# One-hot products of the second layer's further blocks over 128 partitions instead of 32 or 64

## The chip, the cores and the metric

The kernel runs on one core of a Trainium2 chip. The metric is the device time of one execution in microseconds. The weights (about 360 MB read per execution) come from HBM. Engines are named as in the profile: PE is TensorE's matrix products, PEld its loads of the stationary operand, DVE is VectorE, ACT ScalarE, POOL GpSimd, SP SyncE, which issues the weight transfers.

## The reference

A trunk of two layers over 256 latent tokens and 256 context tokens, 1024 channels wide. Each layer mixes tokens (a gated MLP, latent attention and a linear recurrence in parallel), then runs a mixture of 16 experts, and each half ends in a layer norm over alpha * x + gate * sublayer. Only the latent tokens of the second layer's output are returned, so the second layer's experts see 256 tokens. The router picks one group of four experts for a token and two experts in it:

```
best = argmax(group_score); _, local = top_k(in_group, 2)
expert_idx = best * 4 + local;  w = 2.5 * score / sum(score)
out = sum over experts of combine[:, e] * ((silu(h @ wg[e]) * (h @ wu[e])) @ wd[e])
```

The kernel computes each expert for its own tokens alone, all in float32.

## The kernel before

Tokens are sorted by their pair of experts, and a one-hot product gathers them, channel-major, into XgT. An expert's tokens are then a run of at most 256 slots, worked in blocks: slots 0 to 63 always (block 0), then 32, 32, 64 and 64 slots (blocks 1 to 4), each further block only if the expert has that many tokens. This is decided on the chip by a branch (`tc.If` in `over`, L1611) that PE, ACT, DVE and POOL all take. Each block runs through five steps: `take` copies its slots (L1510, L1512), `up` multiplies them with the gate and up weights (L1533), `gate` applies silu and the product (L1539, L1540), `turn` transposes (L1547, L1548), and `down` multiplies with the down weights (L1564). For a block of 32 slots, four groups of 32 columns of the array work side by side in `up` and `down`.

In the second layer the expert's output goes straight back to the tokens. `down` multiplies it with the residual gate (L1578) into rows of a tile y, `place_rows` builds a matrix S (slots by tokens) that holds a token's weight in the row of its slot and zero elsewhere (L1474, L1475), and `scatter` adds S transposed times y to the accumulators cps (L1481): for two token tiles and two halves of the channels, four products of 512 columns. Each is recorded as two instructions, since it is float32. For block 0, two experts share an S of 128 rows, 64 each, and one `scatter` serves both. A further block has its own So and its own y, two tiles named yo; it writes rows 64 up to 64 plus its size, and `scatter` runs over these rows only. So is used once before, by `token_rows`, for the rows of the second layer's weights (L1466, L1467).

PE goes in program order: up products of the next expert (in part), turn and down of this expert, its further blocks inside the branch, the rest of the next expert's up products. `feed` lets SP issue the weight pages (L1284, 1 MB each) into a ring of 16; a page is loaded again when the products that read it before are done. In the profile the tile names of weights are pg and pb, yo appears under its pool's name x, and cps under acc. After the last expert, a layer norm of the accumulators writes the output (L1720 to L1730).

Of the kernel before, what the change touches and what calls it, by code (L numbers as in the profile page):

```python
# [89 lines left out]
def build(tc, I, out, dbg=None):  # L90
    nc = tc.nc
    with ExitStack() as ctx:
        _body(ctx, tc, nc, I, out, dbg or {})


def _body(ctx, tc, nc, I, out, dbg):
# [6 lines left out]
    pe, act, dve, pool, sp = nc.tensor, nc.scalar, nc.vector, nc.gpsimd, nc.sync  # L103
# [14 lines left out]
    def xtile(dt=F):  # L118
        return XP.tile([128, 512], dt, tag="x", name="x")
# [206 lines left out]
    for l in range(NL):  # L326
# [24 lines left out]
        def k2(name="k2", dt=F):  # L351
            return K2.tile([128, 512], dt, tag="k2", name=name)
# [509 lines left out]
        if first:  # L862
# [16 lines left out]
            for q in range(4):  # L879
                h, o = q // 2, q % 2  # L880
                t_ada.append([])
                for i in (1, 0):
                    t = ST.tile([128, 2048], F, tag="adaw", name="adaw", bufs=6)
# [60 lines left out]
        for n in range(2):  # L944
            t = k2("wbd")
# [7 lines left out]
        for n, un in enumerate(units):  # L953
# [15 lines left out]
            if n == LNAT and not first:  # L969
                for m in range(2):  # L970
                    for j, op in ((2, ALU.mult), (3, ALU.add)):
                        t = k2("ln2")
# [319 lines left out]
        if not first:  # L1292
            sc = W2.tile([128, 4, 96], F, name="sc", bufs=1)
            S_ = [W2.tile([128, 256], F, tag="S", name="S") for _ in range(2)]
            So = W2.tile([128, 256], F, name="So", bufs=1)
# [162 lines left out]
        def token_rows():  # L1458

            dve.tensor_tensor(wt[:, 1, :T], wt[:, 1, :T], wt[:, 0, :T], op=ALU.subtract)  # L1460
            for n, (col, dst) in enumerate(((pos, posrow), (wt[:, 0], w0row), (wt[:, 1], wdrow))):
                t = (S_ + [So])[n]
                ps = (yp_[0][:, 0:256], yp_[0][:, 256:512], pt_[0][:, 256:512])[n]
                for a in range(T):
                    s = slice(128 * a, 128 * a + 128)
                    dve.tensor_scalar(t[:, s], ident, col[:, a:a + 1], None, op0=ALU.mult)  # L1466
                    pe.matmul(ps[:, s], onesf, t[:, s], start=True, stop=True, skip_group_check=True)  # L1467
            act.activation(posrow, yp_[0][:, 0:256], AF.Copy)
            act.activation(w0row, yp_[0][:, 256:512], AF.Copy)
            act.activation(wdrow, pt_[0][:, 256:512], AF.Copy)  # L1470

        def place_rows(dst, rows, pcol, fcol):

            dve.scalar_tensor_tensor(dst[rows], wdrow[rows], fcol[rows], w0row[rows], op0=ALU.mult, op1=ALU.add)  # L1474
            dve.scalar_tensor_tensor(dst[rows], posrow[rows], pcol[rows], dst[rows], op0=ALU.is_equal, op1=ALU.mult)  # L1475

        def scatter(S, y, rows, stop=False):
            for i in tiles:
                a = tiles.index(i)
                for n in range(2):  # L1480
                    pe.matmul(cps[i, n], S[rows, 128 * a:128 * a + 128], y[n][rows], start=False, stop=stop,  # L1481
                              skip_group_check=True)
# [7 lines left out]
        else:  # L1490
            gu_ = [sd(), sd()]
            pt_, yp_ = [sd()], [sd()]
            yo = [xtile(), xtile()]
# [20 lines left out]
        def bufs_of(e, b):  # L1514
            q = ORDER.index(e)
            if not first:
                h = slice(64, 128) if b else slice(0, 64)
                return gu_[q % 2], hh_[b % 2 if b else q % 2][h], pt_[0], yp_[0], hT_[min(b, 1)], None
            if b == 0:
                return gu_[q % 2], hh_[q % 2][0:64], pt_[0], yp_[0], hT_[0], y_[q % 2][0:64]  # L1520
            return gu_[2 + b % 2], hh_[b % 2][64:128], pt_[1], yp_[1], hT_[1], y_[(q + b) % 2][64:64 + blocks[b][1]]
# [28 lines left out]
        def down(e, b):  # L1550
            r0, Mb = blocks[b]
            ng = 128 // Mb
            N = 1024 // ng
            _, _, _, yp, hT, y = bufs_of(e, b)
            wd = [streams[l, "wd", e, h].rearrange("p (k c) -> p k c", k=2) for h in range(2)]
            hT3 = hT.rearrange("p (a b) -> p a b", b=64)
            for f in range(4):
                if Mb == 64:
                    lt = hT3[:, f, :]
                else:  # L1560
                    half, c = divmod(f, 2)
                    lt = hT3[:, c, 32 * half:32 * half + 32]
                for j in range(ng):
                    pe.matmul(yp[Mb * j:Mb * j + Mb, :N], lt, wd[f // 2][:, f % 2, N * j:N * j + N],  # L1564
                              start=f == 0, stop=f == 3, skip_group_check=True)
            if not first:
                q = ORDER.index(e)
                if b == 0:
                    rows = slice(64 * (q % 2), 64 * (q % 2) + 64)
                    yt = [y_[q // 2 % 2][:, 512 * n:512 * n + 512] for n in range(2)]  # L1570
                else:
                    rows, yt = slice(64, 64 + Mb), yo
                if b:
                    place_rows(So, rows, pcol[:, b, e:e + 1], fcol[:, b, e:e + 1])
                for j in range(ng):
                    n, c = divmod(N * j, 512)
                    part = slice(Mb * j, Mb * j + Mb)
                    dve.tensor_tensor(yt[n][rows, c:c + N], yp[part, :N], g2[n][part, c:c + N], op=ALU.mult)  # L1578
                if b:
                    scatter(So, yo, rows)  # L1580
                return
            for j in range(ng):
                src, dst = yp[Mb * j:Mb * j + Mb, :N], y[:, N * j:N * j + N]
                if j % 2:
                    dve.tensor_copy(dst, src)  # L1585
                else:
                    act.activation(dst, src, AF.Copy)  # L1587
            if b == 0:
                rows = slice(1024 + ORDER.index(e) * M0, 1024 + ORDER.index(e) * M0 + Mb)
            else:  # L1590
                o, n = (2048, 512) if e % 4 == 3 else (0, 1024)
                rows = ds(nc.values_load(ci[0:1, 1, e:e + 1], engines=[ET.Pool], min_val=0,
                                         max_val=max(n - (r0 - M0) - Mb, 0)) + (o + r0 - M0), Mb)
            st = pool.dma_start(ys[rows, :], y)
            for o in stores:
                tc.declare_no_dep(st.ins, o.ins, reason="other rows")
            stores.append(st)

        def over(e, b, v, following):

            def before(last):
                if last:
                    following()
                if b > 1:
                    turn(e, b - 1)
                down(e, b - 1)

            if b == len(blocks):
                before(True)
                return  # L1610
            with tc.If(v > blocks[b][0], label=f"further_{l}_{ORDER.index(e)}_{b}") as c:  # L1611
                if b + 1 < len(blocks):
                    foretell(ORDER.index(e), v, b + 1)
                wide = b + 1 < len(blocks) and blocks[b + 1][1] == 64
                if b + 1 < len(blocks) and not wide:
                    take(e, b + 1)
                up(e, b, range(8))
                if wide:
                    take(e, b + 1)
                gate(e, b)  # L1620
                before(False)
                over(e, b + 1, v, following)
            with c.Else():
                before(True)
# [46 lines left out]
        for q, e in enumerate(ORDER):  # L1671
# [8 lines left out]
            if q == 0 and not first:  # L1680
                token_rows()
# [237 lines left out]
```

## Time and profile before

| | us |
|---|---|
| median of three timed runs | 1500.34 |
| their lowest and highest | 1496.33, 1503.78 |
| profiled execution, its own time | 1505.39 |
| its span, first to last instruction of the program | 1503.7 |
| PE busy, PEld busy | 1334.2, 843.9 |
| DVE, ACT, POOL busy | 739.6, 449.3, 138.2 |
| second layer's experts, from about / to about | 1225, 1495 |

The profile is of one execution. A row of a timeline merges like instructions that follow each other: start on the span, duration from the first start to the last end, engine, line, operation, output and inputs, shapes and count; in square brackets the time for which the engine was idle before, and what ended it. "issue" stands where nothing that the profile shows was waited for. The granted clock (PEclk) is 1.00 at 2.4 GHz and 0.50 at 1.2 GHz.

### The profile page before, as it was taken

Reading aid. Unit: us, or ns where it says so; the run is one execution under the profiler, and the core shown is the slowest. Engines: PE = TensorE matmul, PEld = TensorE weight load, DVE = VectorE, ACT = ScalarE, POOL = GpSimd, SP = SyncE. Lnnn points to the kernel's source line nnn. Section 1 sums busy time; section 2 is a strip of 40 time slices with the busy share of each in tenths; the row PEclk is TensorE's granted clock in tenths of the full one; section 3 lists DMA queues with packets and bytes.
Section 4 is the critical chain, followed back from the end, with each engine's and each line's share of the span. In section 5 each row is a group of like instructions: output and inputs, shape, how many; then the busy total and the mean of one; then the engine's idle time right before and its main releaser. Section 6 shows DMA issues by size and latency. Waiting matters only on the chain. (4 is left out here: it accounts for less than half of the span.)

```text
span 1503.7 us, 21798 instructions
## 1 busy us (share of the span) xinstructions
PE 1334.2 (89%) x8147; PEld 843.9 (56%) x8147; DVE 739.6 (49%) x1448; ACT 449.3 (30%) x781; POOL 138.2 (9%) x251
## 2 busy tenths in 40 slices
PE   5999889999999978988988779869998889989976
PEld 4777667777787853323333368546767753333322
DVE  3376774553466671323222456887676762222323
ACT  2437533333241221210111173764434320000000
POOL 0020000000022210000000441100002110000000
PEclk9999999999999988998989889999999999898988
DMA  9494332332353377998897646535535579988891
GB/s 377 172 376 173 135 143 89 114 143 85 112 191 118 131 321 300 418 414 346 330 386 280 214 131 231 192 130 200 219 118 205 180 309 403 371 325 340 353 402 49
DMA packets 56816, 358.15 MB, mean 238 GB/s; under 512 B 7316, under 2 KB 8116, under 8 KB 17920
## 3 DMA queue, kind: packets, MB, share of 16 engines
q1 hardware_dynamic: 46048, 320.83, 54.7%
q0 software_dynamic: 9808, 33.39, 6.6%
q8 instruction: 111, 1.82, 0.5%
q10 hardware_dynamic: 720, 1.06, 0.2%
q14 instruction: 129, 1.06, 0.2%
HBM read 342.63 MB, written 12.62 MB: 236 GB/s over the span
## 5 line engine op out<-in xcount | busy, mean ns | idle before, releaser
L373 PE MATMUL acc<-whi,pg 128*128 128x512 f32 (+1 forms) x424 | 173.6, 409 | 0.0
L374 PE MATMUL acc<-wlo,pg 128*128 128x512 f32 (+1 forms) x424 | 165.7, 391 | 4.6 <-DVE wlo L361 4.3
L375 PE MATMUL acc<-whi,pg 128*128 128x512 f32 (+1 forms) x424 | 164.8, 389 | 0.0
L361 DVE TENSOR_TENSOR wlo<-pg,whi 128x1024 fp32r<-128x1024 f32 x104 | 127.0, 1222 | 71.5 <-ACT whi L360 71.2
L360 ACT ACTIVATE whi<-pg 128x1024 fp32r<-128x1024 f32 x104 | 109.5, 1055 | 83.5 <-PE acc L375 54.8
L1564 PE MATMUL sd<-pg,lnv 128*64 128x512 f32 (+1 forms) x416 | 78.0, 566 | 21.2 <-issue 11.0
L374 PEld LDWEIGHTS acc<-wlo,pg 128*128 128x128 f32 x424 | 80.6, 190 | 24.5 <-DVE wlo L361 8.7
L373 PEld LDWEIGHTS acc<-whi,pg 128*128 128x128 f32 x424 | 80.6, 190 | 21.8 <-issue 5.2
L375 PEld LDWEIGHTS acc<-whi,pg 128*128 128x128 f32 x424 | 80.4, 190 | 15.9
L1564 PE MATMUL sd<-pb,lnv 128*64 128x512 f32 (+1 forms) x416 | 70.7, 543 | 14.8 <-ACT lnv L1548 7.1
L1533 PE MATMUL acc<-pg,xs 128*64 128x512 f32 x256 | 71.4, 655 | 13.8 <-DMA pg<-in_wg 4.3
L1539 ACT ACTIVATE hh<-sd 64x512 f32<-64x512 f32 (+1 forms) x18 | 10.2, 568 | 198.7 <-PE sd L1533 198.7
L1533 PE MATMUL acc<-pb,xs 128*64 128x512 f32 x256 | 64.1, 617 | 3.4 <-DMA pb<-in_wu 2.6
L1585 DVE COPY y<-sd 64x512 f32<-64x512 f32 (+1 forms) x32 | 17.9, 558 | 99.6 <-ACT y L1587 83.1
L1533 PE MATMUL sd<-pg,xs 128*64 128x512 f32 x256 | 61.5, 621 | 1.5 <-issue 1.5
L373 PE MATMUL acc<-whi,yhi 128*128 128x512 f32 x144 | 60.3, 419 | 0.0
L1533 PE MATMUL sd<-pb,xs 128*64 128x512 f32 x256 | 59.9, 610 | 0.0
L718 ACT ACTIVATE P<-sd,sm 128x512 f32<-128x512 f32 (+1 forms) x48 | 29.0, 614 | 103.1 <-DVE sm L711 103.1
L1564 PEld LDWEIGHTS sd<-pg,lnv 128*64 128x64 f32 (+1 forms) x416 | 25.4, 135 | 60.3 <-issue 53.9
L375 PE MATMUL acc<-whi,ylo 128*128 128x512 f32 x144 | 57.0, 396 | 0.8 <-DVE ylo L553 0.8
L374 PE MATMUL acc<-wlo,yhi 128*128 128x512 f32 x144 | 56.9, 395 | 0.0
L1533 PEld LDWEIGHTS acc<-pg,xs 128*64 128x64 f32 x256 | 23.3, 149 | 57.6 <-issue 46.0
(470 smaller groups left out, 2378.4 us busy)
## 6 DMA issues: line engine op xcount, KB each, us to landing
pg<-in_win SPq DMA_DIRECT2D x40, 1024.0 KB, 6.0
pg<-in_wada SPq DMA_DIRECT2D x40, 1024.0 KB, 6.2
pg<-in_wg SPq DMA_DIRECT2D x32, 1024.0 KB, 13.6
pg<-in_wu SPq DMA_DIRECT2D x32, 1024.0 KB, 15.5
pb<-in_wd SPq DMA_DIRECT2D x32, 1024.0 KB, 10.0
pb<-in_wg SPq DMA_DIRECT2D x32, 1024.0 KB, 14.3
pb<-in_wu SPq DMA_DIRECT2D x32, 1024.0 KB, 16.4
pg<-in_wd SPq DMA_DIRECT2D x32, 1024.0 KB, 10.3
```

The costliest lines, as they stand in the source:

```text
L360: act.activation(hi, raw, AF.Copy)
L361: dve.tensor_tensor(lo, raw, hi.bitcast(F), op=ALU.subtract)
L373: pe.matmul(ps, ah, bh, start=start, stop=False)
L374: pe.matmul(ps, ah, bl, start=False, stop=False)
L375: pe.matmul(ps, al, bh, start=False, stop=stop)
L718: act.activation(p[:, s], bank[g][:, s], AF.Exp, scale=SCALE, bias=sm[:, 0, i:i + 1], accum_out=sm[:, 1, i:i + 1])
L1533: pe.matmul(gu[Mb * j:Mb * j + Mb, :N], xv[:, k, 0:Mb], w[k // 4][:, k % 4, c:c + N], start=k == 0, stop=k == 7, skip_group_check=True)
L1539: act.activation(hh[:, :N], gu[0:64, :N], AF.Silu)
L1564: pe.matmul(yp[Mb * j:Mb * j + Mb, :N], lt, wd[f // 2][:, f % 2, N * j:N * j + N], start=f == 0, stop=f == 3, skip_group_check=True)
L1585: dve.tensor_copy(dst, src)
```

## The change

`scatter` for a further block now runs over all 128 rows of So and yo. So that the rows outside the block add nothing, POOL clears So and both yo tiles in full once, after `token_rows`, and for a block of 32 slots DVE clears rows 96 to 127 of So each time before `place_rows` (a block of 64 slots writes rows 64 to 127 of So itself). Block 0's products are as they were.

```diff
@@ token_rows
             act.activation(wdrow, pt_[0][:, 256:512], AF.Copy)
+            for t in [So] + yo:
+                pool.memset(t, 0.0)
@@ down
                 if b:
+                    if Mb == 32:
+                        dve.memset(So[96:128], 0.0)
                     place_rows(So, rows, pcol[:, b, e:e + 1], fcol[:, b, e:e + 1])
                 for j in range(ng):
                     n, c = divmod(N * j, 512)
                     part = slice(Mb * j, Mb * j + Mb)
                     dve.tensor_tensor(yt[n][rows, c:c + N], yp[part, :N], g2[n][part, c:c + N], op=ALU.mult)
                 if b:
-                    scatter(So, yo, rows)
+                    scatter(So, yo, slice(0, 128))
```

On PE, ACT and SP the same instructions stand in the same order as before. VectorE's order in the branch that ends a further block of 32 slots, before:

```order
L1611 UNCONDITIONAL_BRANCH
L1667 REGISTER_ALU
L1907 BRANCH_PREFETCH_HINT
L1474 SCALAR_TENSOR_TENSOR So<-moda,sc 32x256
L1475 SCALAR_TENSOR_TENSOR So<-modb,sc,So 32x256
L1578 TENSOR_TENSOR x<-sd,x 32x256 x4
```

And now, in the same branch of VectorE (lines after the first edit have moved by two, later ones by four):

```order
L1615 UNCONDITIONAL_BRANCH
L1671 REGISTER_ALU
L1911 BRANCH_PREFETCH_HINT
L1577 MEMSET So 32x256
L1476 SCALAR_TENSOR_TENSOR So<-moda,sc 32x256
L1477 SCALAR_TENSOR_TENSOR So<-modb,sc,So 32x256
L1582 TENSOR_TENSOR x<-sd,x 32x256 x4
```

One MEMSET has come in ahead of the two operations of `place_rows`; it stands at 64 places of VectorE's program, of which an execution comes to one for each further block of 32 slots that it runs.

GpSimd's order at the first expert of the second layer, before (sc holds the slots' columns, modb the counts):

```order
L1425 IOTA modb 128x1
L1428 MEMSET sc 128x16 x5
L1663 TENSOR_LOAD modb
L1667 REGISTER_ALU
L1907 BRANCH_PREFETCH_HINT
L1663 TENSOR_LOAD modb
L1611 COMPARE_AND_BRANCH
```

And now:

```order
L1425 IOTA modb 128x1
L1428 MEMSET sc 128x16 x5
L1667 TENSOR_LOAD modb
L1671 REGISTER_ALU
L1911 BRANCH_PREFETCH_HINT
L1667 TENSOR_LOAD modb
L1472 MEMSET So 128x256
L1472 MEMSET x 128x512 x2
L1615 COMPARE_AND_BRANCH
```

The three clearings stand between the load of the second expert's count and the first expert's branch.

## Rows read from the trace of the kernel before

**Rows 1.** The profile's page: TensorE's busy time, its clock in 40 slices.
```profile
PE 1334.2 (89%) x8147; PEld 843.9 (56%) x8147; DVE 739.6 (49%) x1448; ACT 449.3 (30%) x781; POOL 138.2 (9%) x251
...
PEclk9999999999999988998989889999999999898988
```

**Rows 2.** TensorE's timeline, first block (start, us, engine, line, op, tiles, count, idle before).
```profile
1299.35 2.77 PE L1564 MATMUL sd<-pb,lnv 128*32 128x256 f32 x32 [1.11 <-DVE y L1578]
1303.09 7.19 PE L1481 MATMUL acc<-x,So 32*128 32x512 f32 x8 [0.96 <-DVE x L1578]
1310.21 8.93 PE L1533 MATMUL sd<-pg,xs 128*64 128x512 f32 x32
...
1320.11 3.65 PE L1564 MATMUL sd<-pg,lnv 128*64 128x512 f32 x16 [0.58 <-issue]
```

**Rows 3.** TensorE's timeline, second block.
```profile
1376.96 1.93 PE L1564 MATMUL sd<-pg,lnv 128*32 128x256 f32 x32 [1.32 <-DVE y L1578]
1379.87 5.01 PE L1481 MATMUL acc<-x,So 32*128 32x512 f32 x8 [0.98 <-DVE x L1578]
1384.81 9.18 PE L1533 MATMUL sd<-pb,xs 128*64 128x512 f32 x32
...
1394.95 3.65 PE L1564 MATMUL sd<-pb,lnv 128*64 128x512 f32 x16 [0.58 <-issue]
```

**Rows 4.** TensorE's timeline, one-hot products over 128 rows and an expert's up products.
```profile
1405.79 3.70 PE L1481 MATMUL acc<-y,S 128*128 128x512 f32 x8
...
1474.20 7.04 PE L1533 MATMUL sd<-pb,xs 128*64 128x512 f32 x32
```

**Rows 5.** The products' line: durations in ns, shortest, median, longest.
```profile
L1481 PE MATMUL acc<-x,So x16: 587/1056/1217, 1303.1 to 1383.8; 32*128 32x512 f32 x16
```

**Rows 6.** Busy time of each engine by stretch, granted clock (PEclk), DMA share.
```profile
1300.40:1303.00 2.60, 1.72 (x19) 0.54 (x8) 0.80 (x2) 0.00 (x0) 0.00 (x0) 0.50 0.95 397
1303.09:1310.21 7.12, 7.12 (x9) 2.50 (x9) 0.83 (x2) 0.00 (x0) 0.00 (x0) 0.50 1.01 422
1310.21:1313.90 3.69, 3.69 (x11) 1.23 (x12) 0.00 (x0) 0.00 (x0) 0.00 (x0) 0.50 0.86 329
1379.90:1382.20 2.30, 2.30 (x6) 0.95 (x7) 0.80 (x2) 0.00 (x0) 0.00 (x0) 1.00 1.01 417
1382.30:1384.80 2.50, 2.50 (x4) 0.49 (x2) 0.00 (x0) 0.00 (x0) 0.00 (x0) 0.50 0.99 419
1384.80:1389.00 4.20, 4.20 (x11) 1.24 (x12) 0.00 (x0) 0.00 (x0) 0.00 (x0) 0.50 1.01 425
```

**Rows 7.** VectorE's timeline around the two blocks.
```profile
1299.24 0.48 DVE L1474 SCALAR_TENSOR_TENSOR So<-moda,sc 32x256 f32<-32x256 f32 x1
...
1302.17 1.78 DVE L1578 TENSOR_TENSOR x<-sd,x 32x256 f32<-32x256 f32 x4 [1.94 <-PE sd L1564]
...
1378.95 1.78 DVE L1578 TENSOR_TENSOR x<-sd,x 32x256 f32<-32x256 f32 x4 [1.12 <-PE sd L1564]
```

**Rows 8.** GpSimd's waits from 1225 us on: total, times, longest.
```profile
POOL pg L1708 <- PE sd L1564: 244.4, 1, 244.4
```

**Rows 9.** SyncE's weight loads (time of issue).
```profile
1310.31 0.33 SPq L1284 DMA_DIRECT2D pb<-in_wu  x1
1321.18 0.80 SPq L1284 DMA_DIRECT2D pg<-in_wd  x2
...
1396.03 0.80 SPq L1284 DMA_DIRECT2D pb<-in_wd  x2
```

**Rows 10.** The same view as rows 6, two stretches ahead of weight loads.
```profile
1315.00:1321.00 6.00, 5.42 (x29) 1.85 (x27) 1.28 (x3) 0.98 (x2) 0.00 (x0) 1.00 0.17 68
1391.50:1396.00 4.50, 3.92 (x22) 1.45 (x20) 1.71 (x4) 0.94 (x2) 0.00 (x0) 1.00 0.17 69
```

**Rows 11.** TensorE's timeline, waits elsewhere.
```profile
1336.53 3.65 PE L1564 MATMUL sd<-pb,lnv 128*64 128x512 f32 x16 [1.89 <-issue]
...
1451.80 3.68 PE L1564 MATMUL sd<-pg,lnv 128*64 128x512 f32 x8 [4.73 <-DMA pb<-in_wg]
```

## The prediction

> **What bounds the kernel now.** I read the page first: TensorE is busy 89% of the span [rows 1], so its queue sets the time unless a stage shows otherwise. The change touches the second layer's experts alone, from about 1225 us to 1495 us, so I then went down TensorE's timeline of that stretch. There it runs one dense chain, expert after expert, and what ends the kernel, the final layer norm, reads what its last one-hot products accumulate. In this execution two experts have more than 64 tokens, and each runs one further block of 32 slots; its down products, 32 records of 32 columns, start at 1299.35 us and at 1376.96 us [rows 2, 3]. Each further block ends with eight matmul records of 32 rows by 512 columns (four products, two records each, since they are float32): 7.19 us for the first, 5.01 us for the second [rows 2, 3]. The same eight records over 128 rows take 3.70 us [rows 4]. The narrow form itself is not slow: the shortest of its 16 records takes 587 ns, the middle one 1056 ns [rows 5].
>
> The granted clock, read in windows cut at the edges of these instructions, gives the reason [rows 6]. Through all of the first block's 32-row products TensorE is busy without a gap (7.12 of 7.12 us), and yet its clock stays at 0.50, that is at 1.2 GHz instead of 2.4. It is still there for the first 3.69 us of the next expert's up products, which are dense and over 128 rows, and is full again after that (those up products take 8.93 us here, 7.04 us at the full clock [rows 2, 4]). Around the second block the clock is full when the 32-row products begin; they run at it for 2.3 us, and then it falls, with TensorE busy all that time, and stays down until 4.2 us into the next up products. So what the 32-row products cost is in the clock, not in their own column count: they let it fall, or keep it down.
>
> **The change, part by part.**
>
> The products over 128 rows. The record count on TensorE is as before, four products per further block; only the partitions are more. At the full clock the products and the 32 up records behind them take 3.70 + 7.04 = 10.74 us [rows 4]. In the first place they take 1310.21 + 8.93 - 1303.09 = 16.05 us, in the second 1384.81 + 9.18 - 1379.87 = 14.12 us [rows 2, 3]. If the clock were full throughout, the gain would be 5.31 us and 3.38 us, 8.69 us in sum. That is the upper bound.
>
> First place: the clock is down already when the products begin (0.50 from 1300.40 us [rows 6]); it fell in the short waits of turn and down before, which the change doesn't touch. Dense 128-row work brought it back after 3.69 us in one place and 4.20 us in the other [rows 6]. While it is down, each microsecond holds half a microsecond of work, so 3.69 to 4.20 us at half clock lose 1.85 to 2.10 us. From the 5.31 us there remain 3.46 to 3.21 us; I take 3.4. It may be more, as some dense work runs at 1300.40 us already, up to the 5.31.
>
> Second place: the clock is full at the start, and of the things that follow only the 32-row products stand where it fell. I take the whole 3.38 us. The lower bound is that it falls here too, in the 0.98 us wait ahead of the products and the 1.32 us before it [rows 3], and then comes back as in the first place: 3.38 - 2.10 = 1.28 us. Lower bound of both together: 3.21 + 1.28 = 4.49 us. Value taken: 6.8 us.
>
> The Trainium skill, "TensorE: Matmul & The Clock Gate", section "Part 1: The HAM clock gate", says that the monitor grants the clock by how busy TensorE has been: sustained matmuls release it, idleness takes it away. By that rule alone the unbroken 32-row products would have released the clock, more rows would change nothing, and the sum would be zero instead of 6.8 us. The trace disagrees in the stretch of 7.12 us, busy throughout at 0.50.
>
> The clearing of the last 32 rows of So, once per 32-slot block on VectorE, two times in this execution. No row shows it; the nearest are the two operations on 32 rows by 256 behind it, about 0.48 us each [rows 7]. A clearing has no input, so I take about half of that, with 0.48 us as the upper bound. It stands ahead of place_rows, and after that VectorE waits 1.94 us and 1.12 us for the block's down product [rows 7]. That wait hides it even at its upper bound. If the wait were gone, it would delay the products by 0.2 to 0.5 us per block, 1 us in all. It needs the earlier readers of So only; they are done long before.
>
> The three clearings on GpSimd, once (So, 128 by 256, and both yo tiles, 128 by 512). They come after the first expert's row products, near 1232 us, and the first reader is the product at 1303.09 us. On GpSimd nothing stands behind them that could be late: its next instruction with work waits 244 us for TensorE [rows 8]. Even 10 us would be hidden, and if they held back VectorE for a moment there, nothing on TensorE's chain is within reach. Cost zero.
>
> What is late next. TensorE's saving counts only if the weights keep up. The issue held back by the products themselves comes right behind them (1310.31 us in the first place); the next group waits for the next expert's down product, at 1321.18 us and, in the second place, at 1396.03 us [rows 9]. Just before these the DMA engines are nearly idle: their share is 0.17 from 1315 to 1321 us and from 1391.5 to 1396 us [rows 10]. So the issues can move up by about 5 us and 3.7 us (the idle 0.83 of each stretch) before the transfers are back to back; 3.4 and 3.4 us fit into that. Everything behind (the weights' issues hang on TensorE, TensorE on itself and on them) moves along, so I pass on the whole saving.
>
> Sum against the profiled execution: 1505.39 - 6.8 = 1498.6 us (span 1503.7 us, with 1.7 us around it). This execution lies 5.05 us above the median of the three timed runs, 1500.34 us. They spread over 7.45 us, which I put down to clock falls at other points in each of them. Taking the same 6.8 us from the median gives 1493.5 us.
>
> **The rivals.**
>
> Rows don't count, or rows of zeros don't: the clock falls in the waits ahead of the products and stays down for a reason other than their 32 rows. For it: both falls come within 4 us of such waits. Against it: ahead of 1336.53 us TensorE waits 1.89 us in one piece [rows 11], longer than the 0.98 us, and the group behind it still takes 3.65 us, as the same group does at 1394.95 us [rows 3] where the clock is back. Zero rows in the moving data appear nowhere else in this stretch, so that part is open. Time: 1500.3 us. Chance 0.1.
>
> The gain is given back by waits for instructions. TensorE has waits that no semaphore explains at 1336.53 us (1.89 us) and 1451.80 us (4.73 us, where the DMA named is no input of the product) [rows 11]; I take them for code that is loaded through busy DMA queues. The branches at 1320.11 us and 1394.95 us, which fall into the two gaps of the DMA, cost 0.58 us each [rows 2, 3]. With narrower gaps one of them may cost 4.73: 6.8 - 4.15 = 2.65 us stay, 1497.7 us. Chance 0.13.
>
> The same on the slow side: the second layer's experts run ahead into saturated DMA queues, so that the branches ahead of the down products wait for code. To be slower by 7.5 us it would have to cost 14.3 us. At 4.15 us each, four branches pay 16.6 us, net 9.8 us slower, 1510.1 us; three (12.45 us) leave the time within 0.5%. It decides from where the DMA gap before both down products vanishes. Against it: of the idle 5 us and 3.7 us the forecast leaves a part. Chance 0.05.
>
> More than the bound: of the kernel's other falls of the clock (every slice at 8 tenths of full speed has one [rows 1]) some that lie behind the blocks go too, since everything there is displaced, or an average execution loses more around the blocks than this one. Some 4 us more than the forecast: 1489.5 us. Chance 0.12.
>
> That the change doesn't do what it says I rule out for TensorE's side: the product takes the whole of So and yo.
>
> **How the numbers follow.** Forecast 1493.5 us with chance 0.6, its own range 1500.34 - 8.69 to 1500.34 - 4.49, 1491.7 to 1495.9 us. A difference of 0.5%, about what a measurement of this kernel can tell from no change, is 7.5 us, so faster means under 1492.8 us. The forecast lies just on the inner side, and a median of three runs that spread over 7.45 us moves, by my estimate, by about 3 us, so four tenths of its chance falls beyond: 0.24. With the 0.12 of the larger gain and a little from the next two, 0.42 faster. Slower: 0.05. Within: 0.53. For the range I add the spread of medians to the forecast's own and take in the larger gain and most of the two cases near 1500: 1487 to 1502 us.
>
> **What would show it.** Right: both groups of one-hot products at So show 128 rows, the one that starts at the full clock takes 3.7 us, and the up products behind each take 7 to 8 us; the granted clock is full within some 4 us of the first group's start, and does not fall in the second. VectorE's clearing ends before the wait for the down product. The next weight issues come 3 to 4 us and 7 us earlier on the span. Wrong: a clock of 0.50 through a whole group of 128-row products; or TensorE shorter there and new waits of 2 to 5 us ahead of later down products.

## The result, and the profile after

The changed kernel takes 1478.49 us (median of four, 1476.84 to 1484.06), the kernel before, timed beside it, 1501.56 us (1496.33 to 1503.78): a ratio of 0.9854, 95% interval 0.9827 to 0.9881, a gain of 23.1 us. The prediction was 1493.5 us, 1487 to 1502: right in sign, far too small. The profiled execution takes 1477.39 us with a span of 1475.6 us, 28.1 us shorter than the one shown of before.

The page of the changed kernel, TensorE's busy time and its clock in 40 slices, against [rows 1]:

```profile
PE 1316.3 (89%) x8147; PEld 841.5 (57%) x8147; DVE 740.5 (50%) x1450; ACT 448.9 (30%) x781; POOL 139.2 (9%) x254
...
PEclk8999999999999989998989989989999999999998
```

The record count is that of before. The slices of 8 tenths near the end have gone, but for the last. The rest is in TensorE's timeline of the changed kernel (start, us, engine, line, op, tiles, count, idle before; the products are at L1483, up L1535, turn L1549, down L1566, and VectorE's multiplication with the gate L1582):

```profile
1213.70 7.09 PE L1535 MATMUL sd<-pg,xs 128*64 128x512 f32 x32 [0.98 <-issue]
...
1297.80 3.73 PE L1483 MATMUL acc<-x,So 128*128 128x512 f32 x8 [1.14 <-DVE x L1582]
1301.46 7.09 PE L1535 MATMUL sd<-pg,xs 128*64 128x512 f32 x32
...
1309.51 3.65 PE L1566 MATMUL sd<-pg,lnv 128*64 128x512 f32 x16 [0.58 <-issue]
...
1323.98 3.65 PE L1566 MATMUL sd<-pb,lnv 128*64 128x512 f32 x16
...
1335.47 3.65 PE L1566 MATMUL sd<-pg,lnv 128*64 128x512 f32 x16 [0.58 <-DMA pb<-in_wg]
...
1346.31 3.70 PE L1483 MATMUL acc<-y,S 128*128 128x512 f32 x8
...
1358.56 0.31 PE L1549 MATMUL sd<-ident,hh 64*128 64x64 f32 x2 [1.37 <-issue]
...
1361.01 2.77 PE L1566 MATMUL sd<-pg,lnv 128*32 128x256 f32 x18 [0.63 <-issue]
1364.90 3.73 PE L1483 MATMUL acc<-x,So 128*128 128x512 f32 x8 [1.12 <-DVE x L1582]
1368.56 7.09 PE L1535 MATMUL sd<-pb,xs 128*64 128x512 f32 x32
...
1376.61 3.65 PE L1566 MATMUL sd<-pb,lnv 128*64 128x512 f32 x16 [0.58 <-issue]
...
1428.53 3.65 PE L1566 MATMUL sd<-pg,lnv 128*64 128x512 f32 x16 [0.58 <-ACTq L1615]
...
1438.27 3.70 PE L1483 MATMUL acc<-y,S 128*128 128x512 f32 x8
...
1461.80 3.70 PE L1483 MATMUL acc<-y,S 128*128 128x512 f32 x8 [0.85 <-DVE y L1582]
```

The counterparts in the kernel before that have no row yet:

```profile
1218.04 7.09 PE L1533 MATMUL sd<-pg,xs 128*64 128x512 f32 x32 [0.98 <-issue]
...
1353.68 1.64 PE L1564 MATMUL sd<-pg,lnv 128*64 128x512 f32 x6 [2.92 <-issue]
...
1364.50 3.70 PE L1481 MATMUL acc<-y,S 128*128 128x512 f32 x8
...
1457.42 3.56 PE L1564 MATMUL sd<-pg,lnv 128*64 128x512 f32 x8 [1.94 <-issue]
...
1467.08 3.70 PE L1481 MATMUL acc<-y,S 128*128 128x512 f32 x8
...
1489.89 3.70 PE L1481 MATMUL acc<-y,S 128*128 128x512 f32 x8 [0.85 <-DVE y L1578]
```

Subtracting the starts of the same work gives where the 28.1 us come from:

| stretch, up to | before, after | lead | gained in it |
|---|---|---|---|
| the experts' first up products | 1218.04, 1213.70 | 4.34 | 4.34, ahead of the change |
| the first block's products | 1303.09, 1297.80 | 5.29 | 0.95 |
| the next down product | 1320.11, 1309.51 | 10.60 | 5.31, products and up |
| the wait of 1.89 us [rows 11] | 1336.53, 1323.98 | 12.55 | 1.95 |
| behind the wait of 2.92 us | 1364.50, 1346.31 | 18.19 | 5.64 |
| the second block's products | 1379.87, 1364.90 | 14.97 | -3.22 |
| the next down product | 1394.95, 1376.61 | 18.34 | 3.37, products and up |
| behind the waits of 4.73 and 1.94 us | 1467.08, 1438.27 | 28.81 | 10.47 |
| the last products | 1489.89, 1461.80 | 28.09 | -0.72 |

The 4.34 us lie ahead of anything that the change touches, and I count them as difference between two executions: in the kept traces of all runs this start lies between 1211.98 us (x3) and 1218.36 us (e0). The other 23.75 us fit the medians. Of them 8.68 are the two blocks with the up products behind them, which is the upper bound of the prediction; 15.1 us lie elsewhere. Four waits that no semaphore explains (1.89, 2.92, 4.73 and 1.94 us) are gone, and with them falls of the clock; a new wait in two pieces (1.37 and 0.63 us) costs 3.22 us with a fall of its own.

The granted clock of the changed kernel in windows (us, busy time of PE, PEld, DVE, ACT, POOL, then PEclk, DMA share, GB/s):

```profile
1297.80:1301.50 3.70, 3.70 (x10) 1.37 (x10) 0.73 (x2) 0.00 (x0) 0.00 (x0) 1.00 1.02 430
1301.50:1308.60 7.10, 7.10 (x35) 2.28 (x35) 0.98 (x2) 0.59 (x1) 0.00 (x0) 1.00 1.01 421
1364.90:1368.60 3.70, 3.70 (x10) 1.37 (x10) 0.73 (x2) 0.00 (x0) 0.00 (x0) 1.00 1.01 425
1368.60:1375.70 7.10, 7.10 (x35) 2.29 (x35) 0.98 (x2) 0.59 (x1) 0.00 (x0) 1.00 0.98 408
1360.70:1364.10 3.40, 2.77 (x18) 0.95 (x18) 0.21 (x1) 0.00 (x0) 0.00 (x0) 0.50 0.94 373
```

In both blocks the products and the up products run at the full clock throughout. One fall is left near the second block, behind its new wait, and it is over before the products begin.

The waits carry falls with them. Two windows of the kernel before, over the pieces of the down group behind 4.73 and 1.94 us:

```profile
1451.80:1455.40 3.60, 3.60 (x8) 0.83 (x8) 0.00 (x0) 0.00 (x0) 1.35 (x2) 0.50 1.01 412
1457.42:1460.80 3.38, 3.38 (x8) 1.00 (x10) 0.00 (x0) 0.00 (x0) 0.00 (x0) 0.51 1.01 373
```

Eight records take 3.56 to 3.68 us there; all sixteen take 3.65 us in the changed kernel, at 1428.53 us.

The trace also shows where the first of the four waits lies: in TensorE's branch instruction ahead of it (count, then shortest, median, longest in ns, and start), in the kernel before:

```profile
L1611 PEldq COMPARE_BRANCH  x1: 6656/6656/6656, 1329.5 to 1329.5; - x1
```

It ends at 1336.2 us, and the products start at 1336.53 us. The same branch takes 1.47 us in the changed kernel. The branch ahead of the wait of 4.73 us takes 6.14 us before and 1.37 us after, and the one ahead of the changed kernel's new wait takes 4.58 us, from 1.99 us before. The waits of 2.92 and 1.94 us lie among the products of a down group, not at a branch.

One more view of the changed kernel, all instructions of the products' line (engine op count: shortest, median, longest in ns; first and last start), has a row that before lacks altogether:

```profile
L1483 PEldq EVENT_SEMAPHORE  x4: 51/51/51, 1297.7 to 1365.7; - x4
```

A semaphore is the counter by which one engine waits for another. TensorE executes two more semaphore instructions in each of the two further blocks, so it does not run the same instructions as before: the view from which that was said of the change does not list them.

### The profile page after: what moved, and what is told of

Its sections match the earlier page's. It is cut to its first block, busy times and chain, and to the rows that moved or that the text cites. A ratio compares the mean times of both kernels' runs of the same rounds, so it can differ in the third digit from the quotient of the medians.

```text
span 1475.6 us, 21812 instructions
## 1 busy us (share of the span) xinstructions
PE 1316.3 (89%) x8147; PEld 841.5 (57%) x8147; DVE 740.5 (50%) x1450; ACT 448.9 (30%) x781; POOL 139.2 (9%) x254
## 5 line engine op out<-in xcount | busy, mean ns | idle before, releaser
L1566 PE MATMUL sd<-pb,lnv 128*64 128x512 f32 (+1 forms) x416 | 70.8, 528 | 17.8 <-ACT lnv L1550 7.5
L1566 PE MATMUL sd<-pg,lnv 128*64 128x512 f32 (+1 forms) x416 | 73.7, 545 | 11.7 <-issue 6.8
L1535 PE MATMUL acc<-pg,xs 128*64 128x512 f32 x256 | 68.2, 636 | 11.4 <-DMA pg<-in_wg 7.5
L1535 PE MATMUL acc<-pb,xs 128*64 128x512 f32 x256 | 62.4, 608 | 3.2 <-DMA pb<-in_wu 2.4
L1535 PE MATMUL sd<-pg,xs 128*64 128x512 f32 x256 | 57.8, 593 | 1.0 <-issue 1.0
L1535 PE MATMUL sd<-pb,xs 128*64 128x512 f32 x256 | 58.1, 593 | 0.0
L1566 PEld LDWEIGHTS sd<-pb,lnv 128*64 128x64 f32 (+1 forms) x416 | 24.6, 129 | 53.0 <-issue 41.7
L1535 PEld LDWEIGHTS acc<-pg,xs 128*64 128x64 f32 x256 | 23.3, 144 | 52.0 <-issue 41.4
```

The costliest lines, as they stand in the source:

```text
L1535: pe.matmul(gu[Mb * j:Mb * j + Mb, :N], xv[:, k, 0:Mb], w[k // 4][:, k % 4, c:c + N], start=k == 0, stop=k == 7, skip_group_check=True)
```

## The experiments

"Added" is what each further block has more on TensorE than before. Ratios are to the kernel before, timed in the same call, with 95% intervals.

| run | rows | added | us | ratio |
|---|---|---|---|---|
| changed kernel | 128 | 2 semaphores | 1478.49 | 0.9854 [0.9827, 0.9881] |
| e1_clears_only | 32 | 2 semaphores | 1487.69 | 0.9928 [0.9902, 0.9955] |
| e2_rows_no_dve_clear | 128 | 2 semaphores | 1479.37 | 0.9872 [0.9852, 0.9892] |
| e3_rows_64 | 64 | 2 semaphores | 1484.16 | 0.9898 [0.9866, 0.9931] |
| x1_pool_three_free | 32 | nothing | 1498.37 | 0.9996 [0.9981, 1.0011] |
| x2_clears_on_dve | 128 | nothing | 1486.92 | 0.9903 [0.9875, 0.9931] |
| x3_pool_one_waiting | 32 | 1 semaphore | 1487.26 | 0.9920 [0.9894, 0.9945] |
| y1_before_pool_out | 32 | nothing | 1498.69 | 1.0000 [0.9979, 1.0021] |
| y2_after_pool_out | 128 | 2 semaphores | 1482.24 | 0.9893 [0.9869, 0.9916] |
| y3_dve_clears_pool_out | 128 | nothing | 1488.32 | 0.9936 [0.9914, 0.9957] |
| z1_pool_held_pe_same | 32 | nothing | 1500.82 | 1.0019 [0.9998, 1.0041] |
| z2_pe_waits_pool_free | 32 | 2 semaphores | 1485.23 | 0.9931 [0.9904, 0.9958] |
| w1_shift_once | 32 | nothing | 1500.55 | 1.0004 [0.9983, 1.0024] |
| w2_split_in_blocks | 32 | a product | 1488.87 | 0.9939 [0.9915, 0.9963] |
| w3_dve_clears_split | 128 | a product | 1480.12 | 0.9863 [0.9835, 0.9891] |
| w4_after_split | 128 | a product, 1 semaphore | 1484.39 | 0.9896 [0.9866, 0.9926] |
| v1_so_pool_yo_dve | 128 | 1 semaphore | 1481.44 | 0.9876 [0.9846, 0.9906] |

**Rows or clears.** Three runs from the changed kernel: the clears without the rows, the rows without VectorE's clear per block, and half of the added rows.

```diff
 e1:                scatter(So, yo, rows)              # instead of slice(0, 128)
 e2: -              if Mb == 32:
 e2: -                  dve.memset(So[96:128], 0.0)
 e3:                scatter(So, yo, slice(64, 128))    # instead of slice(0, 128)
```

> All clearings of the changed kernel, but the products of further blocks over the 32 rows in use, as before. Theory A (what counts is the clock that the 32-row products let fall, and what follows from TensorE's lateness): as before, 1501 us within 5, clock at 0.50 in both blocks. Theory B (the added instructions shift where code is loaded, and the waits of 1.9, 2.9, 4.7 and 1.9 us of the kernel before go by that): about 14 us faster than before, 1487 us, with the clock low in both blocks.

> Products over 128 rows, So and yo cleared once on GpSimd, no clearing on VectorE; VectorE's and TensorE's instructions are as before. Theory A: as the changed kernel, 1478 us within 5. Theory B (shift of the code by VectorE's 64 added instructions): only the clock's share of the gain, 7 to 9 us, 1492 us.

> As the changed kernel, but the products of further blocks run over rows 64 to 127. If half of the rows keeps the clock up as well as all: 1478 us, products at So 3.7 us each. If the clock goes by the rows in use: it holds in a block that starts at the full clock, and does not come back during the products where it starts low; between the two kernels, 1480 to 1492 us. Theory B: 1478 us whatever the clock does.

The clears alone bring 10.8 us, in a kernel whose blocks are as slow as ever: products and up take 15.78 us (1302.71 to 1308.53 + 9.96) in its first block and 14.08 us in its second. e2 leaves the rows outside a block as the last larger block left them and is as fast as the changed kernel within the intervals, so VectorE's clear costs nothing that shows. A fresh execution of the unchanged kernel (e0_before_again, 1503.84 us) had the four waits at the same places, so they aren't chance.

> The kernel before once more, for a second profile. Theory A: low clock in both blocks, and waits of TensorE of 2 to 5 us ahead of later down products, 10 us or more in sum. Theory C (the waits in the first profile were chance): such waits at other places, or under 5 us in sum.

Its first block differs from that of the profile before. The clock is full when the products begin, and falls only then:

```profile
1302.52 5.60 PE L1481 MATMUL acc<-x,So 32*128 32x512 f32 x8 [0.98 <-DVE x L1578]
1308.05 8.58 PE L1533 MATMUL sd<-pg,xs 128*64 128x512 f32 x32
```

Products and up take 14.11 us here, and 14.11 us in its second block too. Against this execution the changed kernel, with 10.75 us in each block, gains 3.36 us twice, 6.72 us, where it gains 8.68 us against the other.

In e3 the two blocks differ. Its TensorE timeline:

```profile
1302.55 3.72 PE L1483 MATMUL acc<-x,So 64*128 64x512 f32 x8 [1.14 <-DVE x L1582]
1306.20 7.09 PE L1535 MATMUL sd<-pg,xs 128*64 128x512 f32 x32
...
1366.18 2.77 PE L1566 MATMUL sd<-pg,lnv 128*32 128x256 f32 x18 [0.90 <-issue]
1370.07 7.16 PE L1483 MATMUL acc<-x,So 64*128 64x512 f32 x8 [1.12 <-DVE x L1582]
1377.16 9.66 PE L1535 MATMUL sd<-pb,xs 128*64 128x512 f32 x32
```

With 64 rows the full clock was held in the first block. In the second it fell behind a wait, as in the changed kernel, but the 64-row products ran at half clock to their end, while the 128-row ones of the changed kernel began at the full clock. So the two second blocks don't compare the numbers of rows; no further block's 128-row group in any kept trace begins at half clock.

**Which clear.** Three instructions on GpSimd that wait for nothing new; the three clears on VectorE; one clear on GpSimd, which waits for TensorE's last reading of So in token_rows.

```diff
 x1 (from before):  for n in range(3):
                        pool.memset(z[:, n], 0.0)      # z is a tile of its own
 x2 (from after):   dve.memset(t, 0.0)                 # instead of pool.memset(t, 0.0)
 x3 (from before):  pool.memset(So, 0.0)
```

> The kernel before, with three small clearings of a tile of its own on GpSimd where the changed kernel has its three, but with nothing to wait for. Theory B1 (GpSimd's three added instructions alone shift code): the four waits of TensorE at the down products of the seventh, eighth and fourteenth expert go, about 1488 us, as in the run with the clearings only. Theory B2 (what matters is that GpSimd waits there until TensorE has read So, and so takes its branches later): no change, 1499 us within 4, the four waits stay.

> The changed kernel with the three clearings of So and yo on VectorE instead of GpSimd, whose instructions are then as before. Theory B1 and B2: only the clock's share of the gain stays, 7 to 10 us, about 1490 us, and the four waits of TensorE are back. If GpSimd has nothing to do with it: 1478 us.

> The kernel before, with one clearing on GpSimd, of So, which waits until TensorE has read it (as the changed kernel's first). Theory B2: about 1488 us, the four waits gone. Theory B1: no change, 1499 us, or a partial one.

More instructions on GpSimd do nothing; one waiting clear brings 12 us (0.992 of 1500) with 32-row products. Without GpSimd's clears the blocks keep their gain (10.77 and 10.78 us in x2, from 16.05 and 14.12), but waits of 2.12, 2.58 and 3.31 us are there. I read this as GpSimd being held back: in before it walked through all branches of the second layer from 1215.7 to 1228.3 us, ahead of TensorE's first at 1230.1 us, and with the waiting clears it does so from 1227.8 to 1239.7 us.

**GpSimd held back: refuted.** It is left out of the second layer's branches.

```diff
-            return nc.values_load(..., engines=BRANCHING, min_val=0, max_val=CAP)
+            return nc.values_load(..., engines=BRANCHING if first else BRANCHING[:3], min_val=0, max_val=CAP)
 (the same in foretell; y1 from before, y2 from after, y3 from x2)
```

> The kernel before with one edit: in the second layer GpSimd takes no part in the experts' branches (no count, no hint, no branch on it); the other three engines and the 32-row products are as before. Theory D (what costs is that GpSimd walks through all the branches of the second layer some 10 us ahead of the other engines, and TensorE's later waits without a semaphore follow from that): the waits ahead of the fourth to sixth experts' down products (2.0 us) and of the 13th's (4.7 us) go as they went with one waiting clear on GpSimd; median 1486 to 1490, ratio near 0.992. Rival E (only the time at which GpSimd starts the walk, against something else that happens between 1215 and 1228 us, or the displaced code of the waiting instruction itself): the four waits stay, median 1496 to 1501. In both the clock still falls around the two further blocks, since the products are those of before.

> The changed kernel (128 rows, clears on GpSimd) with GpSimd left out of the second layer's branches. Theory D: GpSimd's walk was held back already, so nothing more is to be had: 1475 to 1481, no wait over 1.2 us in TensorE's down products. Rival E: likewise 1475 to 1481; a result above 1485 would speak against both and say that the walk in itself is of use when late.

> The changed kernel with the three clears on VectorE instead of GpSimd, which alone measured 1487, and with GpSimd left out of the second layer's branches. Theory D: the 11 us that were lost with the move of the clears come back without any clear on GpSimd: 1475 to 1481, waits gone. Rival E: 1484 to 1489, the first wait of some 2 us still there.

Theory D (GpSimd's early walk costs the time) fails twice: y1 stands at 1.0000 with all four waits, y3 at 1488. y2 comes out at 1482, just above its range. What x3 and the changed kernel have in common and y1, y3, x1, x2 lack is the added semaphore instruction: in these traces a product that depends on VectorE alone has no semaphore instruction ahead of it, and one that depends on GpSimd too has one. The next two runs part the two.

```diff
 z1 (from before):  pool.tensor_copy(z[:, 0], wdrow[:, 0:8])   # z is read by nobody
 z2 (from before):  for t in yo:
                        pool.memset(t, 0.0)
```

> The kernel before with one copy on GpSimd that reads the second layer's weight rows, which ScalarE finishes near 1231 us, and writes a tile that nobody reads. GpSimd is held back as in x3, but no instruction of the other engines gains a wait on it. Theory D' (what counts is that GpSimd is held back): waits of TensorE gone as in x3, median 1486 to 1490, ratio near 0.992. Theory F (what counts is that, with a clear on GpSimd, every further block's one-hot products wait for two engines instead of one, which adds an instruction to TensorE's program in each of the 64 blocks and shifts the code behind it): the four waits stay at 2.0, 2.9, 4.7 and 1.9 us, median 1497 to 1501, ratio 1.000.

> The kernel before with the two yo tiles cleared on GpSimd, without So: GpSimd's clears wait for nothing, so it runs ahead as before, but the one-hot products of each further block (over 32 rows, as before) wait for GpSimd's semaphore as well as VectorE's. Theory D': the four waits stay, median 1497 to 1501. Theory F: the wait ahead of the block's products grows from 0.98 to about 1.1 us by the added instruction, and the waits of 2.0 and 4.7 us ahead of later down products go or move: median 1484 to 1491, ratio near 0.992.

GpSimd's waits in z1 (engine, line, waited for: us in total, times, longest):

```profile
POOL z L1472 <- ACT moda L1471: 22.9, 1, 22.9
```

and in z2:

```profile
POOL x L1472 <- DVE modb L1334: 6.0, 1, 6.0
```

In z1 GpSimd is held as in the changed kernel, till 1231.07 us, and nothing is won; TensorE's timeline has the waits, one of them longer:

```profile
1333.27 3.65 PE L1566 MATMUL sd<-pb,lnv 128*64 128x512 f32 x16 [1.23 <-issue]
...
1349.99 5.66 PE L1566 MATMUL sd<-pg,lnv 128*64 128x512 f32 x16 [5.81 <-issue]
...
1449.49 3.27 PE L1566 MATMUL sd<-pg,lnv 128*64 128x512 f32 x8 [4.58 <-DMA pb<-in_wg]
1454.86 2.95 PE L1566 MATMUL sd<-pg,lnv 128*64 128x512 f32 x8 [2.09 <-DMA pb<-in_wu]
```

In z2 GpSimd runs on from 1215.8 us, and the waits are gone at the same three places:

```profile
1333.32 3.65 PE L1566 MATMUL sd<-pb,lnv 128*64 128x512 f32 x16
...
1344.81 3.65 PE L1566 MATMUL sd<-pg,lnv 128*64 128x512 f32 x16 [0.58 <-DMA pb<-in_wg]
...
1439.51 3.65 PE L1566 MATMUL sd<-pg,lnv 128*64 128x512 f32 x16 [0.58 <-ACTq L1613]
```

z2's line of products has the row of the changed kernel, z1's has none:

```profile
L1483 PEldq EVENT_SEMAPHORE  x4: 51/51/51, 1303.7 to 1373.4; - x4
```

New waits of 0.65 and 0.78 us stand in its second block. So the gain hangs on what the second dependence adds to the blocks, not on when GpSimd runs.

**The wait or the longer code.** Products are split, which adds instructions without a wait: once ahead of all branches, or in each of the 64 further blocks.

```diff
 w1 (from before), token_rows, for So only:
-                    pe.matmul(ps[:, s], onesf, t[:, s], ...)
+                    two products of 64 columns each
 w2 (from before), w3 (from x2), w4 (from after), scatter, for So, the first product only:
-                    pe.matmul(cps[i, n], ..., y[n][rows], ...)
+                    two products of 256 columns each
```

> The kernel before; in token_rows, which runs once ahead of all branches of the second layer, the two products of So are split into two of 64 columns each. TensorE's program gets a few instructions more at one place, so that all of the second layer's branches move by the same amount; no wait is added. Theory F1 (TensorE's later waits depend on where the code of the branches lies, so any added instructions move them): waits change in place or size already here; time anywhere from 1485 to 1505. Theory F2 (it is the added semaphore wait itself that helps): the four waits stay as in before, 1497 to 1501. Theory F3 (it is the length of each block's code that matters, which grows 64 times): also 1497 to 1501 here.

> The kernel before; of the four one-hot products of each further block (over 32 rows as before) the first is split into two of 256 columns. TensorE's program gets a few instructions more in each of the 64 blocks, without any wait. Theories F1 and F3: the waits of 2.0 us ahead of the later down product and of 4.7 us near 1450 go or move, time 1480 to 1495. Theory F2: they stay, 1497 to 1501, or about 0.2 us more for the split.

> The changed kernel with its clears on VectorE (1487 by itself, waits kept), and the first of each further block's products split into two of 256 columns. F1 and F3: the waits go or move as in the run before, 1474 to 1487. F2: 1486 to 1488.

> The changed kernel as it is, and the first of each further block's products split into two of 256 columns, so that each block's code on TensorE is longer once more. F1 and F3: waits change again, up or down, 1470 to 1490, and the place of the 1.4 us wait ahead of the second block's turn changes. F2: as the changed kernel, 1477 to 1480.

w2 changes TensorE's program alone and gains 9 us with products over 32 rows and no added semaphore. Its timeline:

```profile
1328.81 3.65 PE L1567 MATMUL sd<-pb,lnv 128*64 128x512 f32 x16
...
1340.30 3.65 PE L1567 MATMUL sd<-pg,lnv 128*64 128x512 f32 x16 [0.58 <-DMA pb<-in_wg]
...
1436.76 3.65 PE L1567 MATMUL sd<-pg,lnv 128*64 128x512 f32 x16 [3.22 <-issue]
...
1453.62 3.65 PE L1567 MATMUL sd<-pb,lnv 128*64 128x512 f32 x16 [3.43 <-issue]
```

The first two waits are gone, the later ones have other places and sizes. Theory F2 (the semaphore's wait itself helps) falls; that the split lets the products start earlier is worth only 0.23 us in the second block. w1 stays at 1.0004: its wait of 1.9 us has gone too, but those of 2.57, 4.65 and 1.67 us are there. So instructions added inside the blocks change the time (F3), with or without a wait in them, and the same kind added once ahead of the blocks moves a wait and leaves the time. Whether each block's length counts, or how far all the added code together displaces the later ones, isn't told apart: no larger single shift was run. w3 puts the split on x2 and goes from 0.9903 to 0.9863, with intervals that overlap, and keeps waits of 0.93 and 2.62 us; w4 shows that more isn't better, with new waits of 1.53, 2.54 and 1.26 us.

**Half of the added semaphores.** The changed kernel with its yo tiles cleared on VectorE.

```diff
-            for t in [So] + yo:
-                pool.memset(t, 0.0)
+            pool.memset(So, 0.0)
+            for t in yo:
+                dve.memset(t, 0.0)
```

> The changed kernel with the yo tiles cleared on VectorE and only So on GpSimd: one added semaphore instruction on TensorE per further block, as in x3, instead of two. Theory F3 (the length of the blocks' code): waits as in x3, that is a wait of some 3 us within the seventh expert's down products, none ahead of the second block's turn, about 0.9 us near 1430; with the 11 to 12 us of the 128-row products the time is 1487.3 less 11 to 12, so 1474 to 1478. Against it: the changed kernel's own waits (1.4 us ahead of the second block's turn, none in the seventh expert), 1478 to 1481, if the number of added instructions doesn't matter.

Two of the three waits came as in x3 (3.19 us in the same expert's down products, the eighth in order, and none ahead of the second block's turn). The third, about 0.9 us near 1430 us, did not, and a wait of 2.54 us for VectorE stands at 1444.21 us. The time lies above the range of F3 and just above that of its rival, so v1 doesn't decide between them. No run has a lower median than the changed kernel.

## Why the prediction was wrong

**The step that failed** is "The three clearings on GpSimd ... Cost zero". Their time is indeed nothing: they take 0.31 and 0.98 us behind a wait that delays nobody.

```profile
1227.75 0.31 POOL L1472 MEMSET So<- 128x256 f32 x1 [22.41 <-PE sd L1467]
1228.00 0.98 POOL L1472 MEMSET x<- 128x512 f32 x2
```

But I costed the instructions and not what they do to other engines' programs. They make GpSimd a second writer of what TensorE's products read, and each further block that runs executes two semaphore instructions more on TensorE (the program has 64 such blocks), which stand in none of the rows that I compared. With the rows left at 32 the added instructions are worth 10.3 to 12.0 us (z2, e1 and x3, from their ratios at 1500 us).

**The blocks' terms.** The first was sized 3.4 us and measured 5.31, the whole of its upper bound: the clock was full there, since the fall ahead of it, which I took as untouched, did not come in this execution or in e2, e3 and x2. The second was 3.38 and measured 3.37. Together that is 8.68 against 6.8, the smaller part of the error. And the fall ahead of the first block did not come in the unchanged kernel's second profile either, against which the two blocks gain 6.72 us. So the 6.8 us were about right for such an execution, and the 5.31 us come in part from which execution was profiled.

**What held.** Both groups show 128 rows and 3.73 us at the full clock; the up products take 7.09 us. VectorE's clear took 0.27 us ahead of the wait for the down product. The weights kept up: the lead lost between the blocks, 3.22 us, lies at the new wait, whose rows name no transfer.

**The rivals.** "Rows don't count" falls, but by a count and not by one run. In the eight kept traces with 128-row products, all sixteen blocks run at the full clock from the products' start to the end of up, in 10.69 to 11.29 us. In the ten with 32-row products, seventeen of the twenty blocks ran at half clock in part (12.41 to 16.34 us), and three held the full clock, with 10.69 to 10.77 us: the second blocks of x1, x3 and y1, whose products were:

```profile
1379.30 3.75 PE L1484 MATMUL acc<-x,So 32*128 32x512 f32 x8 [0.98 <-DVE x L1581]
1368.02 3.67 PE L1482 MATMUL acc<-x,So 32*128 32x512 f32 x8 [1.07 <-DVE x L1579]
1376.56 3.75 PE L1481 MATMUL acc<-x,So 32*128 32x512 f32 x8 [0.98 <-DVE x L1578]
```

So 32 rows let the clock fall as a rule here, not always, and what decides in those three isn't shown. In them more rows had nothing to gain. The two on waits for instructions named the right waits with the wrong sign, whatever they are for: such waits did change, and those that were there, and were listed in [rows 11], went. A wait that nothing explains was a possible gain as much as a possible cost, and I priced only the cost. "More than the bound" came true in kind, with 4 us above the forecast where 15 came, and from waits rather than falls of the clock alone.

**What doesn't settle.** How the 23 us divide isn't settled, since the parts overlap: rows with nothing added on TensorE give 9.6 to 14.6 us (y3, x2), additions alone 9.2 to 12.0 (w2, z2, e1, x3), both together 15.6 to 21.9 (w4 to the changed kernel). In x2 the last waits shrank too, from 4.73 and 1.94 us to one of 3.31, though no instruction was added on TensorE; VectorE's program is longer there. Why some lengths of code lose the waits isn't shown either. That the waits are for code being loaded is an inference from where they stand, inside branch instructions and behind them with no semaphore open. The instruction queues don't prove it. Before, around the wait of 4.73 us (queue, kind: packets, MB, share of 16 engines' time, 1446 to 1458 us):

```profile
q8 instruction: 2, 0.03, 1.1%
```

The changed kernel, around the same place, where nothing waits (1423 to 1435 us), has the same row to the digit, and one more queue for instructions is alike too (one packet, 0.01 MB).

## What to carry to other kernels

When a change gives a tile a writer on another engine, look at who reads it: each reader now waits for two engines, which added instructions here to a program whose listed work hadn't moved. Waits that no semaphore explains, in code full of branches, changed here with what was added inside the branches; price them both ways, and control a gain by a run that has the same added code without the intended change (e1 and w2 here). A split of the gain by stage, from the starts of the same instructions in two traces, shows at once how much of it lies where the change is; take it against more than one execution of the kernel before, since here the blocks' share was 8.68 us against one and 6.72 us against the other.

## What the runs showed of the hardware

- The clock of dense products went with their number of rows, though not in every case: 32-row products ran 7.12 of 7.12 us busy at 0.50 [rows 6] and held 1.00 in three of twenty blocks, 128-row ones held 1.00 in all sixteen, and 64-row ones held it in one block and, where they began at 0.50, ran 7.13 of 7.13 us at it. The last, in e3:

```profile
1370.07:1377.20 7.13, 7.13 (x10) 2.50 (x10) 0.73 (x2) 0.00 (x0) 0.00 (x0) 0.50 1.01 424
```

- A semaphore instruction on TensorE takes 51 ns by itself; one or two per block, in two blocks that an execution runs, went with 10.3 to 12.0 us (z2, e1, x3), and a split product without any with 9.2 us (w2).
- TensorE's branch instruction ahead of the wait of 1.89 us took 6.66 us, and 1.47 us where the wait was gone.
- The two clears of 128 by 512 that had no product to wait for took 0.98 us on GpSimd together, and one of 128 by 256 0.31 us.
